# A list of experts built by one-hot products instead of a scatter, and the gates' transfers on GpSimd's queue

## The chip, the cores and the metric

One core of one Trainium2 chip runs the whole kernel. The metric is the device time of one execution in microseconds. The engines are TensorE (PE, with its weight loads PEld), VectorE (DVE), ScalarE (ACT), GpSimd (POOL) and SyncE (SP). DMAs are issued from SP's, ACT's or POOL's queue and run on 16 DMA engines; the profile calls the three queues q1, q10 and q0.

## The reference, cut to what matters

Two transformer blocks on 256 tokens of width 2048. The last layer of the second block, `peer`, is the one that the change is in: 8 heads choose 16 of 16,384 experts for each token, weigh them with a softmax, and sum the chosen rows of `v`, each times its gate and times `gelu(x . u)`.

```python
idx = e1 * PEER_NKEYS + e2                      # T x 8 x 16 expert numbers out of 128 x 128
gate = jax.nn.softmax(sc, axis=-1)
h = jax.nn.gelu(jnp.einsum('cd,chkd->chk', xc, u[ic]))
out = jnp.einsum('chk,chkd->cd', gc * h, v[ic])
```

The kernel computes `x . u` for all experts, writes the gates as a dense matrix of experts by tokens, lists the experts that have a gate in either half of the tokens, and then gathers only the listed experts' rows.

## The kernel before, in words

`peer` (L1350) has three stretches.

The first works on 32 groups g of 512 experts (L1513). `fm_group` (L357) takes four units per group; a unit loads 1 MB of `pu` from SP's queue into one of three `raw` buffers (L271), splits it in two halves into a rounded part on ACT (L294) and a rest on DVE (L295), and multiplies both by the tokens in 48 matmuls of 256 columns (L312 to L314). After four units ACT writes the gelu of the group into `ge`, which has two buffers (L1526), and POOL's queue writes `ge` to the DRAM matrix `R` (L1528). POOL's queue has little else to do there until the list is made.

Beside the units runs a list of small pieces of work, `bg`. Every unit adds `rate` to a credit and takes that many pieces from the list (L277 to L281). From g = 6 on the rate is 1.92, for 104 units, and 167 pieces are put on the list: one `turn`, 128 pieces `gates(b, q)` (8 batches b of 16), 6 for the classes and places, 31 `scatter` and one `fetch`.

A piece of `gates` handles two tokens. For each, ACT makes a one-hot matrix of 128 x 128 out of two activations (L1412, L1413), DVE makes two weighted ones (L1415), and one matmul of 256 columns multiplies them (L1417); ACT and DVE then add the halves into the buffer `GB` (L1420, L1421). At the end of a batch (q = 15) ACT's queue issues two DMAs. L1423 writes 128 partitions x 124 experts x 32 tokens to `R`, so 15,872 runs of 128 bytes; L1424 writes the last four experts of each partition to `RD`.

When all batches are done, `classes`, `across`, `within` and `places` compute, for each expert, its place in a list that is sorted by class. `scatter` (L1497) then writes the expert numbers to those places in a DRAM list: 124 indirect DMAs from POOL's queue, each of 128 numbers of 4 bytes. `fetch` (L1505) waits for all of them and loads the list back into SBUF as `L`. The order in which each engine's instructions stand is chosen by a planner that works with the dependencies and its own costs; the scatters and the writes of `ge` share POOL's queue, in order.

The second stretch takes the 4 x 128 experts of `RD` (L1559) in four units that need no list. The third gathers the rows of `R` (L1566) and of `pv` (L1574) by `L`, with indirect DMAs from POOL's queue, for 103 columns of the list.

Of the kernel before, what the change touches and what calls it, by code (L numbers as in the profile page):

```python
# [10 lines left out]
F32R = mybir.dt.float32r  # L11
# [8 lines left out]
P = 128  # L20
# [107 lines left out]
def prep(i):  # L128
    f = np.float32
    out = {}  # L130
    out["x"] = np.ascontiguousarray(i["x"][0].T.reshape(KT, P, T).transpose(1, 0, 2)).reshape(P, KT * T)
    wm = i["w_mod"][0]
    out["wmod"] = np.ascontiguousarray(wm.T).reshape(96, P, D)
    out["c"] = i["c"]
    w = i["w_in"][0]
    o = np.cumsum([0, 256, 256, 512, 512, 16, 1536, 512, 4, 4, 512, 512, 512, 512, 4])
    seg = {n: w[:, o[j]:o[j + 1]] for j, n in enumerate(
        ["gq", "gk", "gv", "gg", "lr", "qkv", "dg", "db", "da", "pu", "fq", "fk", "fv", "ff"])}
    out["win"] = lay(np.concatenate(
        [seg["qkv"], seg["gq"], seg["gk"], seg["gv"], seg["fq"], seg["fk"], seg["fv"], seg["pu"], seg["dg"], seg["gg"]],  # L140
        axis=1))
    sm = np.zeros((D, 128), f)
    sm[:, 0:16] = seg["lr"]
    sm[:, 32:36] = seg["db"]
    sm[:, 64:68] = seg["da"]
    sm[:, 96:100] = seg["ff"]
    out["wsm"] = lay_small(sm)
    out["wlr"] = np.ascontiguousarray(i["gla_w_lr"][0])
    out["poolw"] = np.ascontiguousarray(i["pool_w"][0].transpose(1, 0, 2)).reshape(P, 512)
    out["wout"] = lay(i["w_out"][0])  # L150
    out["wg"] = lay(i["ffn_w_gate"][0])
    out["wu"] = lay(i["ffn_w_up"][0])
    out["wd"] = lay(i["ffn_w_down"][0])
    w2 = i["w_in_2"][0]
    kc, vc, ks, vs, kw, vw = (w2[:, 1024 + 128 * j:1152 + 128 * j] for j in range(6))
    ga = w2[:, 1792:1840].reshape(D, 2, 8, 3)[:, :, :, [1, 2, 0]].transpose(0, 2, 1, 3).reshape(D, 48)
    kb, vb = w2[:, 2864:2992], w2[:, 2992:3120]
    out["wtm"] = np.ascontiguousarray(
        np.concatenate([vs, vw, vb, ga], axis=1).reshape(4, 4, P, 432).transpose(0, 2, 1, 3)).reshape(4, P, 1728)

    def pairs(q):
        return q.reshape(D, 2, 8, 64).transpose(0, 2, 1, 3).reshape(D, 1024)

    out["win2"] = lay(np.concatenate([kc, vc, ks, kw, pairs(w2[:, :1024]), pairs(w2[:, 1840:2864])], axis=1))
    out["wkb"] = lay_small(kb)
    out["w1"] = np.ascontiguousarray(np.stack([
        i[n][0].reshape(16, 2, 64, 128).transpose(1, 2, 0, 3).reshape(P, 2048)
        for n in ("cmp_w1_k_2", "cmp_w1_v_2")]))
    out["w2c"] = np.ascontiguousarray(np.concatenate(
        [i["cmp_w2_k_2"][0], i["cmp_w2_k_2"][0], i["cmp_w2_v_2"][0]], axis=1))  # L170
    wo2 = i["w_out_2"][0].reshape(2, 2, 8, 64, D).transpose(0, 2, 1, 3, 4).reshape(D, D)
    out["wout2"] = lay(wo2)
    out["wq"] = lay(i["peer_wq_2"][0])
    out["fin2"] = i["final_norm_2"].reshape(1, D)
    out["subk"] = np.ascontiguousarray(i["peer_subkeys_2"][0].transpose(2, 0, 1)).reshape(P, 256)
    out["pu"] = lay(i["peer_u_2"][0].T)

    pv = i["peer_v_2"][0].reshape(P, P, D)
    out["pv"] = np.concatenate([pv[:EC].transpose(1, 0, 2).reshape(P * EC, D), pv[EC:].reshape(-1, D)], axis=0)
    out["ids"] = np.arange(P * EC, dtype=np.int32).reshape(P, EC)  # L180
    out["rel"] = np.concatenate([i["rel_bias_2"], np.ones((1, 32), f)], axis=0)
    pos = np.concatenate([np.concatenate([i[n][0].T] * 2, axis=0) for n in ("cmp_pos_k_2", "cmp_pos_v_2")], axis=1)
    v = {
        "bmod": cols(i["b_mod"][0]), "nmix": cols(i["norm_mix"][0]), "nffn": cols(i["norm_ffn"][0]),
        "nfin": cols(i["norm_final"]), "an": cols(i["attn_norm_2"][0]), "fn": cols(i["ffn_norm_2"][0]),
        "glan": cols(i["gla_norm"][0]), "gdnn": cols(i["gdn_norm"][0]),
        "gconv": cols(i["gdn_conv"][0]), "pscale": cols(i["pool_scale"][0]), "fcw": cols(i["ffn_conv_w"][0]),
        "fcb": cols(i["ffn_conv_b"][0]), "alog": rep(i["gdn_a_log"][0]), "dtb": rep(i["gdn_dt_bias"][0]),
        "fbias": rep(i["fox_f_bias"][0]), "sinks": rep(i["sinks_2"][0]), "blr": rep(i["gla_b_lr"][0]), "pos": pos,
    }  # L190
    out["vec"] = np.ascontiguousarray(np.concatenate([v[n] for n, _ in _vec_names], axis=1))
    out["cst"], out["csf"], out["csi"], out["oh"] = constants()
    return {n: np.ascontiguousarray(a) for n, a in out.items()}
# [6 lines left out]
class Model:  # L200
# [1149 lines left out]
    def peer(self):  # L1350
# [6 lines left out]
        XH, XL = self.XH, self.XL  # L1357
        sub = self.t(sp, [P, 2, P])
        nc.gpsimd.dma_start(sub, A["subk"].rearrange("p (a n) -> p a n", a=2))
        ids = self.t(sp, [P, EC], I32)  # L1360
        nc.gpsimd.dma_start(ids, A["ids"])

        R = self.t(self.dp, [P * EC, 2 * T])
        RD = self.t(self.dp, [P, P - EC, T])
        R3 = R.rearrange("(p e) t -> p e t", p=P)
        LIST = self.t(self.dp, [P * EC, 1], I32)
        E1 = self.t(sp, [P, 2, 8, 16])
        E2 = self.t(sp, [P, 2, 8, 16])
        GG = self.t(sp, [P, 2, 8, 16])
# [32 lines left out]
        def gates(b, q):  # L1402
            if q % 16 == 0:
                GB[0] = self.t(sp, [P, P, 32], tag="gb", bufs=2)
            ps = new()
            for j in range(2):
                t = 32 * b + 2 * q + j
                o2 = self.t(sp, [P, P], F32R, tag="o2", bufs=4)
                d2 = self.t(sp, [P, P], tag="d2", bufs=2)
                o1 = self.t(sp, [P, 2, P], F32R, tag="o1", bufs=4)  # L1410

                nc.scalar.activation(d2, iota, AF.Abs, bias=ET[:, 1, t:t + 1])  # L1412
                nc.scalar.activation(o2, d2, AF.Relu, bias=1.0, scale=-1.0)  # L1413
                for k in range(2):
                    nc.vector.tensor_scalar(o1[:, k], iota, ET[:, 0, t:t + 1], GH[:, k, t:t + 1].bitcast(F32),  # L1415
                                            ALU.is_equal, ALU.mult)
                ti.matmul(ps[:, 2 * j * P:2 * j * P + 2 * P], o2, o1, start=True, stop=True)  # L1417
            pv = ps.rearrange("p (j k e) -> p k e j", j=2, k=2)
            gb = GB[0][:, :, 2 * q:2 * q + 2]
            nc.scalar.activation(gb, pv[:, 1], AF.Copy)  # L1420
            nc.vector.tensor_add(gb, pv[:, 0], gb)  # L1421
            if q == 15:
                nc.scalar.dma_start(R3[:, :, T + 32 * b:T + 32 * b + 32], GB[0][:, 0:EC])  # L1423
                nc.scalar.dma_start(RD[:, :, 32 * b:32 * b + 32], GB[0][:, EC:P])  # L1424

                dst = F[:, b // 4] if b % 4 == 0 else F4
                nc.vector.tensor_reduce(dst, GB[0], AX.X, ALU.add)
                if b % 4:
                    nc.vector.tensor_add(F[:, b // 4], F[:, b // 4], F4)
# [3 lines left out]
        FL, M, CN = self.t(sp, [P, 2, EC]), self.t(sp, [P, 4, EC]), self.t(sp, [P, 4])  # L1433
        MT, BT = self.t(sp, [EC, 4, P]), self.t(sp, [P, 8])
        PO, PI, PF = self.t(sp, [P, EC]), self.t(sp, [P, 2, EC], I32), self.t(sp, [P, 2, EC])
        place, bad = self.t(sp, [P, EC], U32), self.t(ep, [P, 1], I32)
        L = self.t(ep, [P, EC], U32)
        got = {}

# [25 lines left out]
        def places():  # L1465
# [13 lines left out]
            nc.vector.tensor_single_scalar(PI[:, 1], PI[:, 0], 7, ALU.logical_shift_right)  # L1479
            nc.vector.tensor_single_scalar(PI[:, 0], PI[:, 0], 127, ALU.bitwise_and)  # L1480
            nc.vector.tensor_copy(PF, PI)

            nc.vector.scalar_tensor_tensor(PO, PF[:, 0], float(EC), PF[:, 1], ALU.mult, ALU.add)
            nc.vector.tensor_copy(place, PO)


            nc.vector.tensor_single_scalar(CN[:, 0:1], BT[:, 5:6], float(KA * P), ALU.is_gt)
# [4 lines left out]
            nc.vector.tensor_copy(bad, CN[:, 0:1])  # L1492


        wrote = []

        def scatter(lo, hi):  # L1497
            for e in range(lo, hi):
                i = nc.gpsimd.indirect_dma_start(LIST, bass.IndirectOffsetOnAxis(ap=place[:, e:e + 1], axis=0),  # L1499
                                                 ids[:, e:e + 1], None)  # L1500
                tc.declare_no_dep(i.ins, group="places", reason="the places are different")
                tc.add_to_no_dep_group("places", i.ins)
                wrote.append(i.ins)

        def fetch():  # L1505
            i = nc.gpsimd.dma_start(L.bitcast(I32), LIST.rearrange("(r c) o -> r (c o)", r=P))
            for w in wrote:
                tc.add_manual_dep(i.ins, w.name, mybir.DependencyInfo(mybir.DependencyClass.Sync, mybir.DependencyReason.DATA),
                                  reason="the list is complete")


        self.rate = 0.5
        for g in range(32):  # L1513
            if g < 4:
                scores(g)
            if g == 6:
                self.bg.append(turn)
                self.bg += [lambda b=b, q=q: gates(b, q) for b in range(8) for q in range(16)]
                self.bg += [classes, lambda: None, across, lambda: None, within, places]
                self.bg += [lambda e=e: scatter(e, e + 4) for e in range(0, EC, 4)]  # L1520
                self.bg += [fetch]
                self.rate = 1.92
            ub = self.fm_group(A["pu"][g], XH, XL)
            ge = self.t(ep, [P, 4, T], tag="ge", bufs=2)
# [196 lines left out]
```

## Time and profile before

| | |
|---|---|
| median of 3 runs | 3310.65 us (3301.16 to 3317.48) |
| the profiled execution | 3312.3 us, span 3310.5 us |
| PE busy | 2990.0 us, 90% of the span |
| DVE, ACT, POOL busy | 65%, 47%, 15% |
| granted TensorE clock, mean | 0.952 of full speed |
| the first stretch from g = 6 on | about 1950 to 2802 us of the span |
| the lowest slices of PE (of 40) | slices 31 and 32, 2483 to 2648 us: 3 and 5 tenths |

A slice is 82.8 us. Busy shares count the time in which an engine executes something; issuing a DMA from ACT's or SP's queue isn't counted as busy. "issue" as a releaser is time in which an engine waited for nothing that the profile shows. Where a line belongs to a helper (L294, L312) the stretch tells which stage it served.

### The profile page before, as it was taken

How to read it: one execution, taken by the hardware profiler on the slowest of the kernel's cores; microseconds unless marked ns; L12 is line 12 of the kernel's file. 1: busy time of each engine (PE TensorE's matmuls, PEld its weight loads, DVE VectorE, ACT ScalarE, POOL GpSimd, SP SyncE). 2: the span in 40 equal slices, each digit the busy share in tenths (PEclk: the TensorE clock that was granted, in tenths of full speed). 3: DMA queues.
4: the chain of work that ended last, by engine and by line, in shares of the span. 5: the costliest groups of instructions: out<-in, count | busy, mean ns of one | idle time of the engine just before them, and what ended most of it. 6: DMA issues, size and time to landing. Idle time of an engine off the chain costs nothing.

```text
span 3310.5 us, 53445 instructions
## 1 busy us (share of the span) xinstructions
PE 2990.0 (90%) x21356; PEld 2781.8 (84%) x21356; DVE 2154.5 (65%) x3842; ACT 1558.8 (47%) x2604; POOL 498.5 (15%) x468
## 2 busy tenths in 40 slices
PE   5989988999999999999999998788883599999998
PEld 4678878999999999887899998788783589777776
DVE  7678987786555555745669977677770134666665
ACT  1163443544444344557554466566550133555545
POOL 3100000000000000200000000000007521556552
PEclk9999999999999999989999999899986799999999
DMA  9955677685655555433345556666661246788886
GB/s 403 386 208 191 216 265 250 218 324 198 245 194 186 183 187 184 163 141 112 129 164 181 183 204 187 177 196 193 181 192 53 96 173 222 263 290 282 299 283 214
DMA packets 253043, 696.66 MB, mean 210 GB/s; under 512 B 149226, under 2 KB 149290, under 8 KB 190832
## 3 DMA queue, kind: packets, MB, share of 16 engines
q1 hardware_dynamic: 75600, 472.29, 40.2%
q0 software_dynamic: 44816, 199.83, 16.8%
q10 hardware_dynamic: 132368, 21.03, 3.6%
q8 instruction: 170, 2.79, 0.3%
q14 instruction: 89, 0.73, 0.1%
HBM read 657.58 MB, written 41.53 MB: 211 GB/s over the span
## 4 chain that ended last, share of the span: by engine, by line
PE 60%; DMA 9%; DVE 8%; issue 7%; ACT 5%; POOL 4%; ACTq 4%; another core or an unknown queue 1%; DVEq 0%; SPq 0%; POOLq 0%
PE t L314 18%; PE t L312 18%; PE t L313 18%; DMA t<-in_wmod 4%; DMA t<-in_pv,t 4%; ACTq L1424 3%; DVE t L295 3%; POOL t L1566 2%; ACT t L294 1%; PE t L310 1%; DVE t L421 1%; PE t L1229 1%; POOL t L1574 1%; ACT t L1260 1%
## 5 line engine op out<-in xcount | busy, mean ns | idle before, releaser
L312 PE MATMUL t<-t,t 128*128 128x256 f32 (+2 forms) x6376 | 1912.8, 301 | 128.6 <-ACT t L294 48.2
L314 PE MATMUL t<-t,t 128*128 128x256 f32 (+2 forms) x6376 | 1905.7, 300 | 42.9 <-DVE t L295 23.8
L313 PE MATMUL t<-t,t 128*128 128x256 f32 (+2 forms) x6376 | 1909.5, 300 | 36.3 <-issue 19.4
L295 DVE TENSOR_TENSOR t<-t,t 128x1024 fp32r<-128x1024 f32 (+2 forms) x938 | 1135.2, 1217 | 808.4 <-ACT t L294 730.0
L294 ACT ACTIVATE t<-t 128x1024 fp32r<-128x1024 f32 (+2 forms) x938 | 982.0, 1052 | 1182.0 <-PE t L313 694.3
L312 PEld LDWEIGHTS t<-t,t 128*128 128x128 f32 x6376 | 1239.3, 194 | 178.6 <-ACT t L294 56.5
L313 PEld LDWEIGHTS t<-t,t 128*128 128x128 f32 x6376 | 1239.8, 194 | 81.4 <-issue 25.7
L314 PEld LDWEIGHTS t<-t,t 128*128 128x128 f32 x6376 | 1237.3, 195 | 83.9 <-DVE t L295 30.2
L421 DVE CUSTOM_DVE_ANT_0 t<-t,t,t 128x1024 f32<-128x1024 f32 x192 | 244.7, 1279 | 59.0 <-DMA t<-in_wmod 58.7
L1415 DVE TENSOR_SCALAR t<-t,t,t 128x128 fp32r<-128x128 f32 x512 | 142.8, 341 | 39.2 <-PE t L1417 39.1
L1574 POOL DMA_INDIRECT t<-in_pv,t x103 | 140.3, 1362 | 179.2 <-DVE t L295 148.1
L1528 POOL DMA_DIRECT2D t<-t x31 | 23.6, 761 | 875.5 <-ACT t L1526 418.5
L1566 POOL DMA_INDIRECT t<-t,t x103 | 137.9, 1339 | 50.7 <-issue 26.8
L1499 POOL DMA_INDIRECT t<-t,t x124 | 126.2, 1018 | 48.0 <-issue 37.5
L310 PE MATMUL t<-t,t 128*128 128x256 f32 (+1 forms) x448 | 116.2, 422 | 13.2 <-ACT t L523 7.1
L310 PEld LDWEIGHTS t<-t,t 128*128 128x128 f32 x448 | 87.5, 197 | 41.8 <-issue 19.7
L1420 ACT ACTIVATE t<-t 128x256 f32<-128x256 f32 x128 | 44.6, 399 | 107.3 <-issue 104.2
L1412 ACT ACTIVATE t<-t,t 128x128 f32<-128x128 f32 x256 | 89.3, 397 | 0.1
L1421 DVE TENSOR_TENSOR t<-t,t 128x256 f32<-128x256 f32 x128 | 49.0, 420 | 60.3 <-ACT t L1420 60.2
L1102 POOL DMA_DIRECT2D t<-in_w2c x1 | 0.6, 564 | 455.3 <-DMA t<-in_win 455.3
L1072 POOL DMA_DIRECT2D t<-in_oh x1 | 0.6, 566 | 454.4 <-PE t L389 454.4
L1417 PE MATMUL t<-t,t 128*128 128x256 f32 x256 | 45.9, 292 | 24.9 <-ACT t L1413 24.8
(393 smaller groups left out, 1821.3 us busy)
## 6 DMA issues: line engine op xcount, KB each, us to landing
t<-in_pu SPq DMA_DIRECT2D x128, 1024.0 KB, 4.8
t<-in_win SPq DMA_DIRECT2D x64, 1024.0 KB, 5.9
t<-in_wmod SPq DMA_DIRECT2D x122, 512.0 KB, 5.9
t<-in_wg SPq DMA_DIRECT2D x44, 1024.0 KB, 4.8
t<-in_wu SPq DMA_DIRECT2D x44, 1024.0 KB, 4.8
t<-in_wd SPq DMA_DIRECT2D x44, 1024.0 KB, 5.0
t<-in_wmod POOLq DMA_DIRECT2D x70, 512.0 KB
t<-in_wout SPq DMA_DIRECT2D x32, 1024.0 KB, 5.4
```

Source lines behind the costliest of these rows:

```text
L294: nc.scalar.activation(h[:, :w], r[:, o:o + w], AF.Copy)
L295: nc.vector.tensor_sub(l[:, :w], r[:, o:o + w], h[:, :w].bitcast(F32))
L310: mm(ps, wh, xh, start=start, stop=stop, skip_group_check=True)
L312: mm(ps, wh, xh, start=start, stop=False, skip_group_check=True)
L313: mm(ps, wh, xl, start=False, stop=False, skip_group_check=True)
L314: mm(ps, wl, xh, start=False, stop=stop, skip_group_check=True)
L421: nc.vector.tensor_tensor_reduce(r, r, self.cb[:, s], 1.0, init, ALU.mult, ALU.add, dst)
L1415: nc.vector.tensor_scalar(o1[:, k], iota, ET[:, 0, t:t + 1], GH[:, k, t:t + 1].bitcast(F32), ALU.is_equal, ALU.mult)
L1424: nc.scalar.dma_start(RD[:, :, 32 * b:32 * b + 32], GB[0][:, EC:P])
L1499: i = nc.gpsimd.indirect_dma_start(LIST, bass.IndirectOffsetOnAxis(ap=place[:, e:e + 1], axis=0), ids[:, e:e + 1], None)
L1566: nc.gpsimd.indirect_dma_start(rt[:, e], None, R, bass.IndirectOffsetOnAxis(ap=L[:, c:c + 1], axis=0))
L1574: nc.gpsimd.indirect_dma_start(r, None, A["pv"], bass.IndirectOffsetOnAxis(ap=L[:, c:c + 1], axis=0))
```

## The change: what it does

The array of expert numbers on the host (`ids`) is replaced by a column with the partition's number (`num`). The DRAM list, `scatter` and `fetch` go. In their place stands `listing`: for each of the 124 expert columns e, ACT makes a one-hot matrix of the place's low part in two activations, DVE makes two weighted matrices of 124 columns (the place's high part, times the partition's number and times e), and one matmul of 248 columns adds their product to one PSUM bank. After the last, ACT and DVE turn the bank into `L`. There are 62 pieces of two columns each, after two empty ones, so that 199 pieces are put on the list at g = 6. The DMAs at the end of each batch of gates go out on POOL's queue, the one to `R` in eight pieces of 16 partitions (1,984 runs of 128 bytes each).

```diff
             if q == 15:
-                nc.scalar.dma_start(R3[:, :, T + 32 * b:T + 32 * b + 32], GB[0][:, 0:EC])
-                nc.scalar.dma_start(RD[:, :, 32 * b:32 * b + 32], GB[0][:, EC:P])
+                for p in range(0, P, 16):
+                    nc.gpsimd.dma_start(R3[p:p + 16, :, T + 32 * b:T + 32 * b + 32], GB[0][p:p + 16, 0:EC])
+                nc.gpsimd.dma_start(RD[:, :, 32 * b:32 * b + 32], GB[0][:, EC:P])
...
-            nc.vector.scalar_tensor_tensor(PO, PF[:, 0], float(EC), PF[:, 1], ALU.mult, ALU.add)
-            nc.vector.tensor_copy(place, PO)
+            nc.vector.tensor_scalar_mul(PF[:, 0], PF[:, 0], -1.0)
...
-        def scatter(lo, hi):
+        def listing(lo, hi):
+            if lo == 0:
+                got["ps"] = new()
             for e in range(lo, hi):
-                i = nc.gpsimd.indirect_dma_start(LIST, bass.IndirectOffsetOnAxis(ap=place[:, e:e + 1], axis=0),
-                                                 ids[:, e:e + 1], None)
...
-        def fetch():
-            i = nc.gpsimd.dma_start(L.bitcast(I32), LIST.rearrange("(r c) o -> r (c o)", r=P))
...
+                o2 = self.t(sp, [P, P], F32R, tag="o2", bufs=4)
+                d2 = self.t(sp, [P, P], tag="d2", bufs=2)
+                o1 = self.t(sp, [P, 2, P], F32R, tag="o1", bufs=4)
+                nc.scalar.activation(d2, iota, AF.Abs, bias=PF[:, 0, e:e + 1])
+                nc.scalar.activation(o2, d2, AF.Relu, bias=1.0, scale=-1.0)
+                nc.vector.tensor_scalar(o1[:, 0, 0:EC], iota[:, 0:EC], PF[:, 1, e:e + 1], self.num, ALU.is_equal, ALU.mult)
+                nc.vector.tensor_scalar(o1[:, 1, 0:EC], iota[:, 0:EC], PF[:, 1, e:e + 1], float(e), ALU.is_equal, ALU.mult)
+                ti.matmul(got["ps"][:, 0:2 * EC], o2, o1[:, :, 0:EC], start=e == 0, stop=e == EC - 1)
+            if hi == EC:
+                nc.scalar.activation(PO, got["ps"][:, EC:2 * EC], AF.Copy)
+                nc.vector.scalar_tensor_tensor(PO, got["ps"][:, 0:EC], float(EC), PO, ALU.mult, ALU.add)
+                nc.vector.tensor_copy(L, PO)
...
-                self.bg += [lambda e=e: scatter(e, e + 4) for e in range(0, EC, 4)]
-                self.bg += [fetch]
+                self.bg += [lambda: None, lambda: None]
+                self.bg += [lambda e=e: listing(e, e + 2) for e in range(0, EC, 2)]
```

## Rows read from the trace of the kernel before

**Rows 1.** The chain of work that ended last, over the whole span, by engine and line, in shares of the span.

```profile
PE t L314 18%; PE t L312 18%; PE t L313 18%; DMA t<-in_wmod 4%; DMA t<-in_pv,t 4%; ACTq L1424 3%; DVE t L295 3%; POOL t L1566 2%; ACT t L294 1%; PE t L310 1%; DVE t L421 1%; PE t L1229 1%; POOL t L1574 1%; ACT t L1260 1%
```

**Rows 2.** Busy time of each engine in stretches of the span (us from its start): busy us of PE, weight loads, DVE, ACT and POOL, with the number of instructions, then the granted TensorE clock, the mean busy share of the 16 DMA engines, and GB/s. The second row holds a whole transfer of a batch of gates, the fourth and fifth lie inside the scatters, the last behind them.

```profile
1990.00:2003.00 13.00, 13.00 (x111) 13.00 (x110) 10.92 (x24) 10.24 (x27) 0.75 (x1) 1.00 0.49 180
2003.00:2020.00 17.00, 6.63 (x56) 6.42 (x54) 7.28 (x12) 1.48 (x4) 0.00 (x0) 0.84 0.92 178
2030.00:2060.00 30.00, 30.00 (x254) 30.00 (x253) 25.03 (x60) 22.80 (x62) 0.75 (x1) 1.00 0.54 193
...
2525.00:2570.00 45.00, 7.29 (x19) 5.68 (x20) 1.23 (x1) 1.06 (x1) 34.34 (x36) 0.50 0.02 0
...
2630.00:2645.00 15.00, 0.00 (x0) 0.00 (x0) 0.00 (x0) 0.00 (x0) 11.60 (x12) 0.50 0.02 0
2690.00:2780.00 90.00, 90.00 (x753) 90.00 (x752) 37.99 (x31) 37.57 (x40) 3.02 (x4) 1.00 0.57 204
```

**Rows 3.** The two DMA issues of a batch of gates on ACT's queue: duration of the issue in ns (least, median, most), the first and last start, and, for L1423, the time from issue to landing.

```profile
L1424 ACTq DMA_DIRECT2D t<-t x8: 13702/13966/14959, 2003.7 to 2448.1; - x8
...
L1423 ACTq DMA_DIRECT2D t<-t x8: 520/521/596, 2003.1 to 2447.5; - x8
...
DMA to landing us min/median/max: 16.7/16.7/16.7
```

**Rows 4.** POOL's instructions in order of time, the writes of `ge` alone (one per group): start, duration, and the idle time before with what ended it. From the first row to the sixth there are 17 intervals, eight of them with a transfer of gates; from the sixth row to the seventh there are four.

```profile
1951.59 0.75 POOL L1528 DMA_DIRECT2D t<-t  x1 [23.11 <-ACT t L1393]
...
2002.06 0.75 POOL L1528 DMA_DIRECT2D t<-t  x1 [24.07 <-ACT t L1420]
2039.60 0.75 POOL L1528 DMA_DIRECT2D t<-t  x1 [36.79 <-ACT t L1420]
2064.43 0.75 POOL L1528 DMA_DIRECT2D t<-t  x1 [24.07 <-ACT t L1420]
...
2433.93 0.75 POOL L1528 DMA_DIRECT2D t<-t  x1 [24.80 <-ACT t L1420]
2470.66 0.75 POOL L1528 DMA_DIRECT2D t<-t  x1 [35.97 <-ACT t L294]
...
2686.37 0.79 POOL L1528 DMA_DIRECT2D t<-t  x1 [7.74 <-ACT t L1526]
```

**Rows 5.** What PE waited for between 1950 and 2480 us: us in total, times, longest.

```profile
PE t L312 <- ACT t L294: 39.8, 8, 10.6
PE t L1417 <- ACT t L1413: 24.8, 4, 7.9
```

**Rows 6.** ACT's DMA queue between 2003 and 2020 us: packets, MB, and the share of the 16 engines' time in this stretch.

```profile
q10 hardware_dynamic: 16416, 2.10, 78.3%
```

**Rows 7.** POOL's groups of instructions over the whole span, by line and shape: busy us, mean ns of one, idle before. L1499 is the scatter; L419 loads 128 runs of 4 KB, L1528 writes 512 runs of 1 KB, L1082 copies 16 x 128 runs of 1.5 KB from DRAM to DRAM.

```profile
L1499 POOL DMA_INDIRECT t<-t,t x124 | 126.2, 1018 | 48.0 <-issue 37.5 <-DVE t L1484 10.5
L419 POOL DMA_DIRECT2D t<-in_wmod x70 | 37.4, 537 | 88.0 <-DMA t<-in_wmod 52.6 <-DVE t L421 15.8 <-DVE t L541 6.1
L1528 POOL DMA_DIRECT2D t<-t x31 | 23.6, 761 | 875.5 <-ACT t L1526 418.5 <-ACT t L1420 397.9 <-ACT t L294 36.0
...
L1082 POOL DMA_DIRECT2D t<-t x2 | 2.1, 1036 | 22.0 <-DMA t<-t 22.0
```

**Rows 8.** Busy time in two stretches while a transfer of L1082 runs (columns as in Rows 2).

```profile
880.00:890.00 10.00, 10.00 (x88) 10.00 (x87) 5.75 (x8) 3.95 (x4) 0.00 (x0) 1.00 1.01 364
890.00:900.00 10.00, 10.00 (x87) 10.00 (x86) 5.42 (x7) 3.69 (x4) 1.03 (x1) 1.00 0.90 333
```

**Rows 9.** The scatters on POOL in order of time, the first and the last of the stretch in which POOL issues them without a longer pause, the first after the pause, and the last of all; then what PE waited for between 2480 and 2720 us.

```profile
2481.96 1.07 POOL L1499 DMA_INDIRECT t<-t,t  x1 [10.54 <-DVE t L1484]
...
2570.54 0.97 POOL L1499 DMA_INDIRECT t<-t,t  x1 [0.30 <-issue]
...
2594.24 0.99 POOL L1499 DMA_INDIRECT t<-t,t  x1 [0.30 <-issue]
...
2675.22 0.97 POOL L1499 DMA_INDIRECT t<-t,t  x1 [0.30 <-issue]
...
PE t L312 <- issue: 46.8, 20, 25.3
PE t L313 <- issue: 19.4, 17, 2.4
PE t L314 <- issue: 18.5, 19, 2.5
```

**Rows 10.** One-hot matrices in the gates' stretch: durations of the two activations and of the DVE operation in ns (least, median, most); and, in the chain, 64 matmuls of 128 columns with operands that aren't rounded.

```profile
L1412 ACT ACTIVATE t<-t,t x256: 383/396/423, 1952.0 to 2440.5; 128x128 f32<-128x128 f32 x128
...
L1413 ACT ACTIVATE t<-t x256: 290/305/327, 1952.6 to 2441.0; 128x128 fp32r<-128x128 f32 x128
...
L1415 DVE TENSOR_SCALAR t<-t,t,t x512: 328/341/354, 1953.1 to 2441.0; 128x128 fp32r<-128x128 f32 x171
...
2802.84 7.15 PE t L1544 x64
```

**Rows 11.** The instruction that frees the first scatter; the first gather by the list; and a gather's transfer in the chain.

```profile
2481.44 0.23 DVE L1484 CAST t<-t 128x124 uint32<-128x124 f32 x1
...
2783.31 1.02 POOL L1566 DMA_INDIRECT t<-t,t  x1 [4.03 <-PE t L314]
...
2787.20 5.04 DMA t<-t,t
```

More of the change, by code (lines that the diff above doesn't have):

```diff
@@ L179, in prep @@
     out["pv"] = np.concatenate([pv[:EC].transpose(1, 0, 2).reshape(P * EC, D), pv[EC:].reshape(-1, D)], axis=0)
-    out["ids"] = np.arange(P * EC, dtype=np.int32).reshape(P, EC)
+    out["num"] = np.arange(P, dtype=f).reshape(P, 1)
     out["rel"] = np.concatenate([i["rel_bias_2"], np.ones((1, 32), f)], axis=0)
@@ L1359, in peer @@
         nc.gpsimd.dma_start(sub, A["subk"].rearrange("p (a n) -> p a n", a=2))
-        ids = self.t(sp, [P, EC], I32)
-        nc.gpsimd.dma_start(ids, A["ids"])
+        self.num = self.t(sp, [P, 1])
+        nc.gpsimd.dma_start(self.num, A["num"])
         R = self.t(self.dp, [P * EC, 2 * T])
@@ L1365, in peer @@
         R3 = R.rearrange("(p e) t -> p e t", p=P)
-        LIST = self.t(self.dp, [P * EC, 1], I32)
         E1 = self.t(sp, [P, 2, 8, 16])
@@ L1435, in peer @@
         PO, PI, PF = self.t(sp, [P, EC]), self.t(sp, [P, 2, EC], I32), self.t(sp, [P, 2, EC])
-        place, bad = self.t(sp, [P, EC], U32), self.t(ep, [P, 1], I32)
+        bad = self.t(ep, [P, 1], I32)
         L = self.t(ep, [P, EC], U32)
@@ L1492, in places @@
             nc.vector.tensor_copy(bad, CN[:, 0:1])
-        wrote = []
-        def scatter(lo, hi):
+        def listing(lo, hi):
+            if lo == 0:
+                got["ps"] = new()
             for e in range(lo, hi):
-                i = nc.gpsimd.indirect_dma_start(LIST, bass.IndirectOffsetOnAxis(ap=place[:, e:e + 1], axis=0),
-                                                 ids[:, e:e + 1], None)
-                tc.declare_no_dep(i.ins, group="places", reason="the places are different")
-                tc.add_to_no_dep_group("places", i.ins)
-                wrote.append(i.ins)
-        def fetch():
-            i = nc.gpsimd.dma_start(L.bitcast(I32), LIST.rearrange("(r c) o -> r (c o)", r=P))
-            for w in wrote:
-                tc.add_manual_dep(i.ins, w.name, mybir.DependencyInfo(mybir.DependencyClass.Sync, mybir.DependencyReason.DATA),
-                                  reason="the list is complete")
+                o2 = self.t(sp, [P, P], F32R, tag="o2", bufs=4)
[10 more added lines that the diff above has]
+                nc.vector.tensor_copy(L, PO)
         self.rate = 0.5
```

## The prediction

> **What bounds the kernel now.** I read the chain of waits first: PE's three product lines hold 54% of it, and the one line that is no engine's work and no load is ACT's queue at L1424, 3%, about 100 us [rows 1]. So the kernel is PE's almost everywhere, and the question is where PE isn't fed. The windows answer that. Undisturbed, PE is full: 753 matmuls in 90 us, 0.120 us each, so a group of 192 takes 23.0 us [rows 2]. Two things break this between 1950 and 2690 us.
>
> The first is the end of each batch of gates. While ACT's queue issues its two transfers, ACT is busy 1.5 of 17 us and PE 6.6 [rows 2]. The issue of L1424 holds ACT's queue for 13.97 us, eight times; L1423 in front of it takes 0.52 us to issue but 16.7 us to land [rows 3]. The splits and one-hots stand behind it on ACT, and PE waits for just these: 39.8 + 24.8 us [rows 5].
>
> The second is the scatters, 2482 to 2676 us. In 45 us of that PE executes 19 matmuls, DVE and ACT one instruction each, the DMA engines are 2% busy and the granted clock is 0.50 of full, the lower level of 1.2 GHz; in another 15 us nothing but POOL works [rows 2]. PE's waits there are put down to "issue", 84.7 us in all, so the profile names no producer [rows 9]. But PE is full again in the pause between 2571 and 2594 us, and after the last scatter. I take the scatters for the cause, whatever the path.
>
> **The change, part by part.** All sums are against the profiled execution, 3312.3 us; the median of the runs is 1.7 us lower, which is nothing here.
>
> *Transfers off ACT's queue.* Seventeen intervals between writes of `ge` take 2470.66 - 1951.59 = 519.1 us; an undisturbed one takes 2064.43 - 2039.60 = 24.83 us and one with a transfer 37.5 or 36.7 [rows 4]. 519.1 - 17 x 24.83 = 97 us, 12.1 us per transfer, is what the issues cost. The waits of [rows 5], 64.6 us, are the lower bound; the rest is the half clock after a wait. What replaces it on POOL: nine issues per batch. The nearest row for a piece of 16 x 124 runs is L1082, 16 x 128 runs, 1.04 us; 128 runs cost 0.54 and 512 runs 0.76 us [rows 7]. So 8 x 1.04 + 0.76, with 0.3 us between them as between scatters, is some 12 us. A batch has 16 pieces of work, 8.33 units of 5.75 us, plus 3.8 us for its own matmuls, 51.7 us, in which POOL has else only two writes of `ge`. The pieces wait for DVE's last addition; behind them on POOL stands only the next write of `ge`, and as `ge` has two buffers it has some 50 us before anyone needs the buffer.
>
> The bytes remain. ACT's queue used 78.3% of 16 engines over 17 us, 13.3 us [rows 6]; the units and `ge` use 0.54 [rows 2], 28 us of 51.7. Sum 41 of 51.7 us, and a transfer that yields to the loads takes 13.3 / 0.46 = 29 us. A like load is on record: while L1082 moves 3 MB on POOL's queue, the engines are 0.90 to 1.01 busy and PE is full at clock 1.00 [rows 8]. I leave 0.5 us per transfer for late loads: **-93 us**; bounds -97 and 0.
>
> A rule speaks against this. The Trainium skill, "DMA: Bandwidth & Descriptors", section "Issuing engines are not separate DMA queues", says that transfers from any engine end on the same 16 DMA engines, and that issuing elsewhere saves only the sequencer's time, usually small beside the transfer. Here that sequencer time is 14 us per batch by the trace, so by the row the sum has -93; by the rule's "usually small" it would have about nothing, the first rival below.
>
> *Scatter and fetch go.* From 2470.66 to 2686.37 us are four intervals, 215.7 us [rows 4], where undisturbed groups need 92. With 1.5 us for the places' own matmuls, **-122 us**. Lower bound: the 84.7 us of "issue" waits.
>
> *Listing.* 124 times two activations, two DVE operations and a matmul of 248 columns: a gates' token without the closing additions. ACT is 0.76 and DVE 0.83 busy with gates running undisturbed while PE is full [rows 2], and listing asks less of both (0.40 and 0.31 us for activations, 2 x 0.34 us on DVE, before overlap [rows 10]), so only PE pays. A gates' piece costs (24.83 - 23.0) / 7.68 = 0.24 us, 7.68 being pieces per group; 62 pieces cost 15 us. No rounded matmul under 256 columns is in the trace: by unrounded ones, 7.15 / 64 = 0.112 us per 128 columns [rows 10], 124 would cost 27 us, by 248 / 256 of 0.120 us 14.4. I take **+15 us**, nearest to its own twin.
>
> *Waits.* The first listing needs `PF`, at DVE's end of the places (the old path's last step there is at 2481.4 [rows 11]), one unit after their start. In order on PE, a late one-hot holds the units up: **+2 us**, bounds 0 and 6.
>
> *The end of the list.* 199 pieces at 1.92 per unit take 103.6 of 104 units, so `L` is ready only in the last unit, where before the first gather went out at 2783 us, some 19 us before the groups' end. After the loop come 64 transposes (7.15 us [rows 10]) and four units without list, 96 products of 512 columns at twice a unit matmul's time, 23 us. Four gathers at 1.3 us and 5.0 us of transfer [rows 11], a product and a split of 3.5 us: 14 us after `L`, under that cover of 30. Cost 0; without the cover up to 14 us.
>
> Sum: 3312.3 - 93 - 122 + 15 + 2 = **3114 us**.
>
> **Rivals.**
>
> *The transfer is not hidden.* PE stalled because 16,000 small packets fill the DMA engines (0.92 busy [rows 2]), and ACT's queue only showed it. Then loads starve wherever the issue stands: 3114 + 93 = 3207 us. For it: that share. Against: PE's waits name ACT, none a load [rows 5], and [rows 8].
>
> *POOL becomes the bound, slower than before.* If a run of 128 bytes costs POOL what one of a scatter's costs, 1.018 us / 128 = 8 ns [rows 7], a piece takes 16 us and a batch 127 us against 51.7. The last batch would be out at 2003 + 8 x 127 = 3019 us. The gathers of `R` need it; before, they could have begun as late as 2802 + 30 - 14 = 2818 us, with 494 us to follow. So 3513 us. It decides at (2818 - 2003) / 8 = 102 us per batch, 12.7 us per piece. Against it: L1082's 2048 runs in 1.04 us.
>
> *The stall wasn't the scatters'.* The profile names no releaser for it [rows 9]; if it stays with listing in their place, 3114 + 122 = 3236 us. Against: it ends and begins again with them.
>
> *The list comes late:* ACT and DVE don't keep up beside the last units and the cover is lost: 3114 + 14 + 6 = 3134 us.
>
> **How the numbers follow.** Forecast 0.76, transfer not hidden 0.10, late list 0.05, the stall stays 0.04, POOL the bound 0.05. The forecast's own range, from the bounds of listing, waits and sharing, is 3095 to 3145. The range reaches to the first rival: 3092 to 3210, leaving out the stall's and POOL's cases and part of the forecast's tails. About 0.5% is what a measurement of this kernel can tell from no change. Only POOL's case is slower, 0.05; one of its half-way sizes would give no change, 0.01; faster 0.94.
>
> **What would show it.** Right: no issue of ACT's queue over 1 us between 1950 and 2500; writes of `ge` some 25 us apart through all batches, and the same through listing; pieces near 1.0 us on POOL; no "issue" waits of PE behind the places; PE clock near 1.00 throughout; the first gather at the loop's end, near 2605 us. Wrong: PE waiting for L294 behind loads that land late (first rival); POOL busy without a pause from 2003 on (second); PE waits on listing's one-hots, or a gap at the end before the gathers' products.

## The result, and the profile after

On one chip the kernel before took 3314.07 us (median of 4 runs) and the changed one 3188.91 us (4 runs, 3180.66 to 3193.48): ratio 0.962, 95% interval 0.9578 to 0.9663. That is faster and inside the range, but 75 us above the forecast of 3114. The profiled execution took 3180.7 us (span 3178.7), 67 us above it. PE's busy time is the same (2994.2 us, 94% of a shorter span); what went is idle time, and some that should have gone stayed.

The stretches that answer to [rows 2]: a transfer, the end of that transfer, the list, and the last groups (columns as there).

```profile
2003.00:2020.00 17.00, 17.00 (x145) 16.98 (x144) 16.97 (x30) 10.71 (x28) 9.25 (x10) 1.00 1.00 214
2020.00:2030.00 10.00, 10.00 (x84) 9.80 (x83) 7.38 (x21) 8.34 (x24) 0.79 (x1) 1.00 0.94 292
...
2400.00:2450.00 50.00, 40.78 (x136) 31.07 (x135) 49.56 (x202) 45.98 (x187) 0.00 (x0) 0.54 0.19 52
...
2560.00:2600.00 40.00, 40.00 (x336) 40.00 (x335) 17.16 (x14) 16.07 (x18) 1.51 (x2) 1.00 0.58 209
```

In the first row PE is full where it was 6.6 of 17 us before, though the DMA engines are 1.00 busy. The third row is the surprise: for 50 us PE executes 136 matmuls, some 2.7 per us in place of 8.4, at a granted clock of 0.54 (close to the lower of its two levels, 1.2 GHz), while DVE is busy 0.99 and ACT 0.92 of the time.

POOL in order of time, which answers to [rows 3] and [rows 4]: the first write of `ge` there, a batch's pieces, then the writes from the last batch of gates on, and the loop's last.

```profile
1952.11 0.75 POOL L1528 DMA_DIRECT2D t<-t  x1 [23.12 <-ACT t L1392]
...
2003.89 8.12 POOL L1423 DMA_DIRECT2D t<-t  x8 [0.52 <-DVE t L1420]
2011.99 0.78 POOL L1424 DMA_DIRECT2D t<-t  x1
...
2372.32 0.76 POOL L1528 DMA_DIRECT2D t<-t  x1 [20.48 <-ACT t L1419]
...
2453.88 0.79 POOL L1528 DMA_DIRECT2D t<-t  x1 [59.11 <-ACT t L1502]
2476.11 0.77 POOL L1528 DMA_DIRECT2D t<-t  x1 [21.44 <-ACT t L1526]
2515.84 0.75 POOL L1528 DMA_DIRECT2D t<-t  x1 [38.95 <-ACT t L1526]
2538.28 0.75 POOL L1528 DMA_DIRECT2D t<-t  x1 [21.69 <-ACT t L1526]
...
2653.27 0.75 POOL L1528 DMA_DIRECT2D t<-t  x1 [22.29 <-ACT t L1526]
```

In the kernel before, the loop's last write stands here:

```profile
2778.53 0.75 POOL L1528 DMA_DIRECT2D t<-t  x1 [22.29 <-ACT t L1526]
```

Eight pieces and the one to `RD` take 8.9 us of POOL, and no longer queue stands. But two intervals between writes of `ge` are 81.6 and 39.7 us, where an undisturbed one is 23.0. PE's own order there (start, duration, wait):

```profile
2450.21 0.79 PE L1505 MATMUL t<-t,t 128*128 128x248 f32 x2 [0.19 <-ACT t L1502]
2451.19 0.79 PE L1505 MATMUL t<-t,t 128*128 128x248 f32 x2 [0.20 <-ACT t L1502]
2452.18 0.79 PE L1505 MATMUL t<-t,t 128*128 128x248 f32 x2 [0.19 <-ACT t L1502]
2453.15 0.58 PE L312 MATMUL t<-t,t 128*128 128x256 f32 x1 [0.19 <-ACT t L1526]
```

The planner did not spread the list over the units. 98 of its 124 matmuls stand in one block up to 2453 us and 26 in a second from 2500 us, with no unit's matmul between them. In a block PE has hardly anything else to do (32 of the transposes that follow the loop, L1544, were put into the first), so it runs at the pace of the one-hots, two columns in 0.98 us, at the lower clock. The waits, of PE and then of ACT, from 1950 to 2660 us (us in total, times, longest):

```profile
PE t L1505 <- ACT t L1502: 11.0, 39, 3.5
PE t L314 <- DVE t L295: 6.0, 9, 1.3
```

```profile
ACT t L294 <- DMA t<-in_pu: 34.0, 9, 5.8
...
ACT t L1501 <- DVE t L1482: 6.8, 1, 6.8
```

Of the waits of [rows 5] 2.7 of 39.8 and 1.2 of 24.8 us are left, and the "issue" waits of [rows 9] are gone, but the units' splits now wait 34.0 us for loads. The DMA view of 2003 to 2030 us shows why (packets, MB, share of 16 engines; KB and us to landing):

```profile
q0 software_dynamic: 785, 2.54, 58.3%
q1 hardware_dynamic: 548, 3.99, 39.1%
...
t<-in_pu SPq DMA_DIRECT2D x4, 1024.0 KB, 11.6
```

POOL's queue takes 58% of the engines, and a unit's load lands after 11.6 us, where it takes 4.9 between 2560 and 2640 us.

### The profile page after: what moved, and what is told of

Read it like the earlier page. It is cut to its first block, busy times and chain, and to the rows that moved or that the text cites. A ratio compares the mean times of both kernels' runs of the same rounds, so it can differ in the third digit from the quotient of the medians.

```text
span 3178.7 us, 54489 instructions
## 1 busy us (share of the span) xinstructions
PE 2994.2 (94%) x21480; PEld 2781.7 (88%) x21480; DVE 2214.3 (70%) x4091; ACT 1621.0 (51%) x2853; POOL 439.2 (14%) x415
## 5 line engine op out<-in xcount | busy, mean ns | idle before, releaser
L1566 POOL DMA_INDIRECT t<-t,t x103 | 134.3, 1304 | 52.8 <-issue 29.6
L1528 POOL DMA_DIRECT2D t<-t x31 | 23.7, 765 | 796.8 <-ACT t L1526 480.1
L1423 POOL DMA_DIRECT2D t<-t x64 | 64.8, 1033 | 57.9 <-DVE t L1420 32.6
L1412 ACT ACTIVATE t<-t 128x128 fp32r<-128x128 f32 x256 | 65.9, 308 | 6.8 <-PE t L1416 6.8
L383 DVE TENSOR_TENSOR t<-t,t 128x1024 fp32r<-128x1024 f32 (+3 forms) x62 | 61.4, 1013 | 2.7 <-ACT t L382 2.6
L1505 PE MATMUL t<-t,t 128*128 128x248 f32 x124 | 47.9, 480 | 12.1 <-ACT t L1502 11.0
```

The source lines that it names most:

```text
L1566: nc.gpsimd.indirect_dma_start(rt[:, e], None, R, bass.IndirectOffsetOnAxis(ap=L[:, c:c + 1], axis=0))
```

## Experiments

They ran in four groups, each on a chip of its own. The kernel before took 3280.5, 3282.4, 3308.5 and 3282.0 us there, so ratios are compared within a group. The intervals quoted are those between writes of `ge`, as in [rows 4]. Nine of them run from the write behind the seventh transfer to the loop's end, and undisturbed these would take 24.8 + 8 x 23.0 = 208.8 us. They took 344.6 us before and 281.0 us after.

### First group: the two halves, and the order (before: 3280.46 us)

**Transfers alone.** The kernel before with the diff's first hunk only; the scatters stay.

> The kernel before with only the gates' transfers moved to GpSimd's queue in eight pieces; scatter and fetch stay. If each transfer still costs some 3 us by late loads (the writes of ge stand 22.9 us further apart over 16 groups than undisturbed ones in the changed kernel), 8 x (12.1 - 3) = 73 us go: 0.978 of before. If the transfers cost nothing any more, 97 us go: 0.971. If they are not hidden at all: 1.000. In all three the stretch of the scatters keeps its 122 us and PE's waits for nothing that the profile names.

3181.66 us, ratio 0.9688 (0.9663 to 0.9712). The first sixteen intervals sum to 421.1 us, as after (420.2). The scatters start at 2409.7 us, and PE is full beside them for more than 100 us (columns as in [rows 2]), with no "issue" wait at all. Instead there is one long wait:

```profile
2410.00:2520.00 110.00, 110.00 (x920) 110.00 (x919) 46.54 (x38) 45.50 (x47) 83.22 (x74) 1.00 0.61 206
```

```profile
PE t L312 <- ACT t L294: 51.3, 1, 51.3
PE t L312 <- ACT t L1527: 7.5, 1, 7.5
```

So on this chip the scatters' price has another cause than the one I read from [rows 9]. The gain of 98.8 us is above the 73 that I expected: the transfers gave about what was expected, and the rest came from the scatters' stretch, where the kernel before has a wait of 93.0 us on such a chip (second group).

**Listing alone.** The changed kernel with both transfers on ACT's queue as before.

> The changed kernel with the gates' transfers back on ACT's queue, so only the list is made in the new way. The planner puts the 124 listing matmuls in groups of four between the units here, where in the changed kernel it puts 98 of them in one block. If the block is what makes the list dear, listing costs 15 to 17 us here: 122 - 17 = 105 us less than before, 0.968. If listing costs some 66 us wherever it stands (two activations per column on ACT, 0.49 us, 124 times): 122 - 66 = 56 us less, 0.983. If the stall was not the scatters', it stays: 1.00 or more.

3203.26 us, ratio 0.978 (0.9753 to 0.9808). Here the planner spread the list in groups of four matmuls. The writes of `ge` (on POOL, as above) through it:

```profile
2493.62 0.75 POOL L1527 DMA_DIRECT2D t<-t  x1 [23.09 <-ACT t L1501]
2518.46 0.75 POOL L1527 DMA_DIRECT2D t<-t  x1 [24.09 <-ACT t L1501]
2543.31 0.76 POOL L1527 DMA_DIRECT2D t<-t  x1 [24.10 <-ACT t L1501]
```

24.8 us each; eight such intervals cost 197.3 - 184 = 13 us, a little under the 15 to 17 expected. The gain of 77.2 us is still not the 105 expected, for that took the 122 us of the first profile: on a chip without "issue" waits the four intervals with scatters take 188.4 us (2480.00 to 2668.40 in the next group's profile of the kernel before), 96 and not 124 above full groups. The halves gave 98.8 and 77.2 us, 176 in sum, where both together, in the next run, gave 138.

**List in program order.** The changed kernel, with the list's matmuls told to the planner as fixed in the order of the program.

```diff
-                ti.matmul(got["ps"][:, 0:2 * EC], o2, o1[:, :, 0:EC], start=e == 0, stop=e == EC - 1)
+                i = ti.matmul(got["ps"][:, 0:2 * EC], o2, o1[:, :, 0:EC], start=e == 0, stop=e == EC - 1)
+                tc.keep_in_program_order(i)
```

> The changed kernel, with each listing matmul held behind the matmul that stands before it in the program, an order without a wait: groups of four between the units instead of one block of 98 and one of 26. If the block is the cause, PE stays at full clock through it and some 49 us go: 3140 us, 0.948 of before. If ACT's two activations per column set the pace wherever they stand, no gain: 3189 us, 0.962.

3142.41 us, ratio 0.9581 (0.9565 to 0.9597). The nine last intervals, whose first and last write follow, fall from 281.0 to 234.8 us, and through the list PE is full at the upper level of its clock (columns as in [rows 2]):

```profile
2372.83 0.76 POOL L1529 DMA_DIRECT2D t<-t  x1 [21.64 <-ACT t L1419]
...
2607.60 0.75 POOL L1529 DMA_DIRECT2D t<-t  x1 [23.86 <-ACT t L1502]
```

```profile
2458.00:2583.00 125.00, 125.00 (x1051) 125.00 (x1050) 82.35 (x192) 83.99 (x201) 3.62 (x6) 1.00 0.52 185
```

What is left in the trace: PE's longest wait from 1950 to 2660 us, and ACT's for loads:

```profile
PE t L312 <- ACT t L382: 9.3, 1, 9.3
```

```profile
ACT t L294 <- DMA t<-in_pu: 31.9, 8, 5.0
```

The first stands behind the loop: `L` is ready at 2627 us, the load of `RD` stands on POOL among gathers that wait for `L`, and the first units without list wait for `RD`. The second is the late loads.

**Pieces apart.** The changed kernel, the nine DMAs of a batch sent one at a time beside the next batch's work, each made to wait for that piece's addition on DVE.

```diff
-                    nc.gpsimd.dma_start(R3[p:p + 16, :, T + 32 * b:T + 32 * b + 32], GB[0][p:p + 16, 0:EC])
+                    late.append((R3[p:p + 16, :, T + 32 * b:T + 32 * b + 32], GB[0][p:p + 16, 0:EC]))
...
-            nc.vector.tensor_add(gb, pv[:, 0], gb)
+            done = nc.vector.tensor_add(gb, pv[:, 0], gb)
+            if q % 2 or b == 0 or q == 0:
+                send(done)
```

> The changed kernel, with the nine transfers of a batch issued one at a time beside the next batch's pieces of work, some 5 us apart, instead of all at once. If loads come late because the transfers fill the DMA engines for 20 to 30 us at a time, the waits for loads (34 us on ACT in the gates' stretch) go and some 20 us with them: 3169 us, 0.956 of before, as long as the block of listing stays as it is. If the bytes cost the same wherever they are put: 3189 us, 0.962.

3269.41 us, ratio 0.9962 (0.9943 to 0.9982): a miss. The loads are on time now, but PE waits for the gates' one-hots, and every second interval is 43.8 us:

```profile
ACT t L294 <- DMA t<-in_pu: 3.4, 1, 3.4
```

```profile
PE t L1424 <- DVE t L1422: 35.4, 31, 5.2
```

But only the first batch's pieces went out some 6 us apart (2014.8 to 2058.5 us). There PE is full and no split waits for a load (in after a split waits 4.1 us for one beside the same batch, at no cost to PE):

```profile
2005.00:2055.00 50.00, 50.00 (x419) 49.86 (x418) 45.12 (x93) 37.42 (x96) 9.66 (x10) 1.00 0.85 222
```

The nine of a later batch stand within some 20 us (2108.0 to 2127.3), beside gates that are bunched in the same way, and as PE waits there, a single load is issued between 2107 and 2135 us. So that spreading the burst cures the late loads is seen for one batch only; this way of spreading it costs more than it saves.

### Second group: the scatters' price, and two attempts to gain more (before: 3282.38 us)

**Before again**, unchanged.

> The kernel before, unchanged, profiled on the chip of these runs. It tells whether PE's 84.7 us of waits put down to "issue" are there in every profile of this kernel or were a matter of one chip. If they come from the scatters: 75 to 95 us again, between the first and the last scatter. If they were an accident of one execution: near 0, and the span some 60 to 80 us shorter than 3310.

3284.48 us, span 3282.7. Not one "issue" wait; PE is full beside the scatters (first line) until it stops for one long wait. PE's waits between 2480 and 2720 us:

```profile
2500.00:2550.00 50.00, 50.00 (x419) 50.00 (x418) 21.87 (x18) 21.24 (x23) 39.33 (x37) 1.00 0.55 189
```

```profile
PE t L312 <- ACT t L294: 93.0, 1, 93.0
PE t L314 <- DVE t L295: 0.5, 1, 0.5
```

ACT in order of time, and the last scatter on POOL:

```profile
2559.38 1.06 ACT L294 ACTIVATE t<-t 128x1024 fp32r<-128x1024 f32 x1 [1.82 <-PE t L313]
2659.59 0.33 ACTq L1540 DMA_DIRECT2D t<-in_fin  x1
2660.02 2.95 ACT L294 ACTIVATE t<-t 128x1024 fp32r<-128x1024 f32 x3 [99.59 <-DMA t<-t,t]
```

```profile
2657.28 0.96 POOL L1499 DMA_INDIRECT t<-t,t  x1 [0.30 <-issue]
```

ACT stands for 99.6 us and moves 2 us after the last scatter. In front of its split the planner had put L1540, the load of the final norm's weights, which waits for the last scatter (I take it that its memory is what the scatters' operands occupy until then). The program has it behind the loop; on ACT's queue it stands six groups ahead of the loop's end.

**Scatters later.** The kernel before, with 20 empty pieces of work ahead of the scatters.

```diff
+                self.bg += [lambda: None] * 20
                 self.bg += [lambda e=e: scatter(e, e + 4) for e in range(0, EC, 4)]
```

> The kernel before with 20 empty pieces of work in front of the scatters, so that the first one goes out some 10 units (60 us) after the places are done, and some 100 us after ACT's last issue of L1424, instead of some 20. If scatters alone hold PE up: the waits put down to issue move with them, 75 to 95 us, time unchanged within 10 us. If they hold it up only close behind ACT's last transfers: under 20 us of such waits and a time some 60 us shorter.

3282.75 us. It tells little: the planner moved the scatters forward again (the first at 2482 us), and the trace shows the same wait of 93 us.

**Pinned and apart.** Pieces apart, with the list's and the gates' matmuls both in program order.

> The list in program order (as in the run before), the gates' matmuls in program order too, and the transfers of a batch sent one piece at a time beside the next batch's pieces of work. If the late loads behind the bursts cost the 3 us per transfer that they seem to: PE's splits wait under 5 us for loads in place of 32, and 3142 becomes 3118 to 3125. If the bytes cost the same however they are sent, 3142. If the planner moves the work again, as in the run with the pieces apart, over 3160.

3241.68 us, ratio 0.9875 (0.9856 to 0.9894): a miss, with the intervals of 43.8 us again and the same wait (34.9 us, 31 times) on the one-hots. So PE's order is not what makes them late. What does was not settled. In both runs a batch's one-hots are bunched: in pieces apart 24 of 32 matmuls stand between 2199 and 2217 us, beside nine pieces, and none between 2226 and 2271. A candidate that no run tested is the buffer `GB`, of which there are two: one is free only when its batch's pieces have left, and these now leave beside the next batch.

**Rate 2.0.** The list in program order, with `self.rate = 2.0` in place of 1.92.

> The list in program order, and 2.0 in place of 1.92 pieces of work per unit, so that 199 pieces end after 100 of 104 units, 4 units (24 us) sooner. If the wait of 9.3 us at the end of the groups is the list's lateness: it goes, 3130 to 3135. If the gathers are held by POOL's queue or the load of RD: the wait stays and 3142. If ACT and DVE can't keep up with 2.0: more PE waits on one-hots, 3150 or more.

3159.5 us, ratio 0.9638 (0.9616 to 0.9661). Half a hit: PE's wait at the loop's end shrinks as expected, but ACT's for loads grows from 31.9 us:

```profile
PE t L312 <- ACT t L382: 0.9, 1, 0.9
```

```profile
ACT t L294 <- DMA t<-in_pu: 58.3, 14, 6.4
```

The nine last intervals are 7.7 us shorter than in program order at 1.92, the sixteen before them, with the transfers, 18.7 us longer.

### Third and fourth group: the norm's load (before: 3308.47 and 3282.0 us)

**Norm's load moved.** The kernel before, one word changed.

```diff
-        nc.scalar.dma_start(w, A["fin2"].to_broadcast([P, D]))
+        nc.gpsimd.dma_start(w, A["fin2"].to_broadcast([P, D]))
```

> The kernel before with one word changed: the load of the final norm's weights (L1540) is issued on POOL's queue, behind the scatters, in place of ACT's, where it stands between the splits six groups before the loop's end and needs memory that the last scatter frees. If this issue is what PE waits for (93 us in one wait on ACT's split in the second profile of the kernel before): that wait goes. POOL still has the writes of ge queued behind blocks of 25, 43, 42 and 14 scatters of 1.27 us, so that the third write goes out some 140 us after the first scatter and the group that needs its buffer is some 30 us late: 3282 becomes 3215 to 3225. If POOL's queue costs nothing beside it: 3190. If the scatters themselves hold PE up: 3282.

3302.68 us, ratio 0.9982 (0.9959 to 1.0005): no difference, against my expectation. But on this chip the "issue" waits of [rows 9] are back (2480 to 2720 us):

```profile
PE t L312 <- issue: 35.0, 31, 5.0
PE t L313 <- issue: 31.1, 27, 3.1
PE t L314 <- issue: 21.2, 19, 2.4
```

**The same kernel again**, on the fourth group's chip.

> The kernel before with the norm's load on POOL's queue once more, since the chip of the last run made PE creep during the scatters (87 us of waits put down to issue), which hides what the load's issue costs. Where the kernel before takes about 3280 (no creeping, one wait of 93 us): 3215 to 3225 if the issue on ACT's queue is the cause and POOL's order the rest, 3280 if neither is. Where it takes about 3310: 0.998 of it again, and the waits put down to issue in the trace again.

3252.41 us, ratio 0.9912 (0.9881 to 0.9943): 30 us gained, half of what I expected. No "issue" waits, no wait for the norm's load, and in its place (PE's waits, then ACT in order of time):

```profile
PE t L312 <- ACT t L1526: 57.1, 3, 31.6
```

```profile
2583.91 0.60 ACT L1526 ACTIVATE t<-t 128x512 f32<-128x512 f32 x1 [20.87 <-DMA t<-t]
...
2640.14 0.60 ACT L1526 ACTIVATE t<-t 128x512 f32<-128x512 f32 x1 [33.53 <-DMA t<-t]
```

ACT's gelu waits for a `ge` buffer, that is for a write of `ge` that stands on POOL's queue behind a block of scatters.

**Scatters without the norm's load** (third group). The transfers on POOL in eight pieces, the scatters kept, the norm's load on POOL.

> The transfers on POOL in eight pieces, the scatters kept, and the norm's load on POOL's queue. With the transfers alone the time was 3181 and one wait of 54 us stood behind the norm's load. If that is the cause: 54 us less 10 to 20 for POOL's queue, 3135 to 3150, no slower than the list by products in program order (3142). If scatters cost PE time whatever waits behind them: 3181.

3206.46 us, ratio 0.9662 (0.9607 to 0.9718): a miss, with 55.9 us of "issue" waits on this chip (2400 to 2720 us). PE creeps here although neither the gates' transfers nor the norm's load stand on ACT's queue, and not throughout: beside the first scatters it is full for 36 us, of which this is a part:

```profile
2420.00:2440.00 20.00, 20.00 (x169) 20.00 (x169) 8.49 (x7) 7.94 (x9) 15.75 (x15) 1.00 0.64 233
```

One of its four runs took 3174.94 us; whether PE crept in it too, no trace tells.

**RD early** (third group). The list in program order, a buffer of its own for `RD`, loaded on SP's queue.

```diff
-                gd = self.t(ep, [P, 4, T], tag="ge", bufs=2)
-                nc.gpsimd.dma_start(gd, RD)
+                gd = self.t(ep, [P, 4, T], tag="gd", bufs=1)
+                nc.sync.dma_start(gd, RD)
```

> The list in program order, with a buffer of its own for RD and its load on SP's queue in place of POOL's, where it stood behind gathers that wait for the list. If the wait of 9.3 us at the end of the groups was for RD: it goes, 3130 to 3136. If it is the list's lateness: PE waits a few us later for the gathers' split instead, and 3142. If SP's loads of the units stand behind it: slower than 3142.

3141.94 us, ratio 0.9511 (0.948 to 0.9543), the best ratio because the kernel before took longest on that chip; by its own time it equals the list in program order (3142.41 on another chip). The wait of 9.3 us is gone, and one of 3.3 us for the gathers stands in its place:

```profile
PE t L314 <- DVE t L383: 3.3, 1, 3.3
```

The profiled span is 3132.8 us against 3140.0. Whether the 7 us are real, its runs (3134.58 to 3154.27) don't decide.

## Why the prediction was right or wrong

From the first write of `ge` in [rows 4] to the loop's last, 25 intervals, the sum meant 826.9 - 93 - 122 + 15 + 2 = 629 us. After took 701.2 us (1952.11 to 2653.27), 72 us more; outside the stretch it gained 6 us that no term had. The 72 us lie in two terms.

**Listing, +15: the step that failed.** The work was sized well: spread, it costs 13 us (listing alone). But the step took over from its twin that it would be spread, at 1.92 pieces per unit beside full units. The planner put it in blocks, where PE waits for one-hots, a sign of being wrong that the prediction had named, and runs at the lower clock (0.54 granted). From the write at 2372.32 us on, after took 281.0 us where the sum meant 24.8 + 92 + 1.5 + 17 + 92 = 227.3: 54 us missing. In program order 46 of them come back, so this is shown, though on another chip (a full group takes the same 23.0 us there, and the sixteen intervals before take 424.9, 4.7 more). Why the planner makes blocks here and not in listing alone, no run tells. I had reckoned the engines' shares and never asked who sets the order; [rows 4] and the gates' matmuls showed only the order that the planner chose for other pieces.

**Transfers, -93: right in kind, the rest for late loads mis-sized.** A piece takes 1.03 us against 1.04 from L1082, and the waits of [rows 5] are nearly gone. The transfer is hidden but for (420.2 - 16 x 24.83) / 7 = 3.3 us each, seven transfers lying in these sixteen intervals, in place of my 0.5; some 19 us in all. My 41 of 51.7 us averaged over a batch; the nine DMAs go out in 9 us and fill the engines until about 2030. That they fill them, and that a load then lands after 11.6 us, is in the trace of after. That sending them apart cures the loads is seen for one batch; the fall of the waits from 34.0 to 3.4 us in the whole of that run doesn't show it, since PE needed fewer loads there. The Trainium skill, "DMA: Bandwidth & Descriptors", section "Issuing engines are not separate DMA queues", is half borne out: transfers issued on POOL's queue do share the 16 engines with SP's loads, at 3.3 us each; but the issue, whose time it calls usually small beside the transfer, held ACT's queue for 13.97 us beside a transfer of 16.7, and without it the sixteen intervals are 62 us shorter (482.3 to 420.2).

**Scatter and fetch, -122: about the right size on that chip, for an incomplete reason.** Before, 124 us of the intervals went to them, and none of it is in after; where PE doesn't creep they took 96. But "PE stalls because scatters run" is one of three things behind the same 167 to 194 us on POOL: the norm's load on ACT's queue (a wait of 93.0 us on a chip where PE doesn't creep), behind it the writes of `ge` in POOL's order (57.1 us with that load moved), and on some chips the creeping of PE (84.7 and 87.3 us of "issue"). They overlap, so taking one away gains 30 us or nothing. [Rows 9] showed only the creeping, because it hid most of the other two. Two lines of the same profile that the prediction left out speak against "it ends and begins again with them": PE is full for 12 us beside eight scatters after the pause (columns as in [rows 2]), and ACT waits 14.08 us behind the norm's load.

```profile
2594.00:2606.00 12.00, 12.00 (x103) 12.00 (x102) 4.90 (x4) 4.23 (x4) 9.59 (x8) 1.00 0.66 236
```

```profile
2677.98 2.95 ACT L294 ACTIVATE t<-t 128x1024 fp32r<-128x1024 f32 x3 [14.08 <-DMA t<-t,t]
```

The two halves don't add either: with the transfers on POOL, the nine intervals with scatters take 279.2 us, 70 above the undisturbed, where before had 344.6, 124 above and 12 more for the eighth transfer. On that chip the list in place of the scatters was then worth 3181.66 - 3142.41 = 39 us, in program order. In blocks, as the change has it, the kernel took 3188.91 us on its own chip, where the transfers alone took 3181.66 on this one: as far as two chips compare, the blocks ate what the list had gained.

**Waits, +2, and the end of the list, 0.** At the head of the block ACT waits 6.8 us for `PF`, and PE 3.5 us for ACT, inside the bounds of 0 and 6. The end cost nothing in after, where the blocks made the list early; with the list spread it cost 9.3 us of wait, inside the bound of 14. The cover that I counted on began with `RD`'s product, and I had not looked at what stood ahead of its load on POOL.

**The rivals.** "The transfer is not hidden" holds for about a quarter (3.3 of 12.1 us each). POOL is not the bound (8.9 us per batch, where it decided at 102). "The stall wasn't the scatters'" is wrong as a forecast, since the stall went with the scatters, and right as a doubt about the view: no releaser named meant that the cause wasn't known. "The list comes late" came true in the version in program order.

## What to carry to other kernels

Where a planner orders the engines, a piece of work costs what its place costs: ask which rows show that the planner will spread it, and pin the order if none does. An indirect DMA that frees memory or shares a queue holds up everything that was planned early behind it, a load that nobody needs yet included; look for the issue that stands just ahead of the waiting instruction. And a stall put down to "issue" is an open question: profile it on a second chip before building a term on it.

## What was not expected of the hardware

The same program behaved differently in profiles taken on different chips. While scatters run, PE creeps on some: 19 matmuls in 45 us, at the lower clock, with the DMA engines 0.02 busy ([rows 2], [rows 9], and both kernels with scatters of the third group), though there too it is full beside scatters for stretches of 12 to 36 us. On the other chips PE is full beside the same scatters at nearly the same pace (37 in 50 us in before again, where the creeping stretch has 36 in 45), for over 100 us with the transfers alone. Each group ran on its chip at one time only, so that it is the chip, and not something that passes, isn't shown. The creeping does not need transfers on ACT's queue, nor the norm's load there. What it is stays open: no trace names a releaser, and no run settled it.
